# A hybrid decoder layer: a later column addition, last products by halves, and tiles copied by GpSimd's transfers ahead of their transposes

## The chip, the core and the metric

One core of a Trainium2 chip. The time is device microseconds of one launch, the median of the runs shown; one further execution was profiled, and all rows here are from it. Engines are named as in the profile: PE is TensorE's matmuls, PEld its weight loads, DVE VectorE, ACT ScalarE, POOL GpSimd, SP the engine that issues the loads.

## What is computed

One decoder layer on 512 tokens of width 1024, all in float32:

```python
mod = silu(c) @ w_mod + b_mod          # six vectors of 1024: shift, scale, gate, twice
h = rms_norm(x) * (1 + sc_m) + sh_m
proj = h @ w_in                        # q, k, v of two mixers, indexer inputs, two gates
q_a, k_a, q_b, k_b = rope(rms_norm(...))      # 4 heads of 128 each
o_a = attention over the 128 keys that an indexer picks (top-k), causal
o_b = block-sparse attention, causal
merged = sigmoid(gate_a) * (o_a @ w_br_dsa) + sigmoid(gate_b) * (o_b @ w_br_moba)
x = x + gt_m * (merged @ w_out)
h = rms_norm(x) * (1 + sc_f) + sh_f
x = x + gt_f * ((silu(h @ w_gate) * (h @ w_up)) @ w_down)
```

## The kernel before

Products keep float32's precision in three float32r matmuls each: both operands are split into a high and a low part (`wh`, `wl`; tiles of tag `H`, `O`, `K`, `g`), and `mm3` (line 152) adds high x high, high x low and low x high into one PSUM bank. Weights come from DRAM on SP's queue into `st` tiles (`wload`, line 163); ACT makes the high part and DVE the low one.

After the first stage (to about 66 us), the program is written out by a planner that runs when the kernel is built. `Clocks` (line 50) keeps, for each engine, the time that it expects, and for each tile the time at which it should be ready. The main line is a list of chunks of weights (`drive`, line 578; `group`, line 550), whose matmuls go out in a fixed order; after each three of them `step` (line 497) looks at the other tasks, generators that yield what they wait for, and issues what the clocks say is ready by PE's planned time. Engines run their instructions in the order so made, and wait on semaphores where a tile is late in fact.

The tasks that matter here:
- `post` (line 673), one for each of 16 tiles (queries and keys of both mixers, 4 tiles of 128 tokens; tiles `g`): root mean square on ACT, rope on DVE, a power on POOL (`rstd_of`, line 254), the scaling by ACT, 4 transposes on PE by the identity into a PSUM bank (`pstr`), and a copy by ACT into `K`. The tile is float32, and so are its transposes.
- `head` (line 851), one for each mixer, query tile and head: scores (PE, `pss`), mask and maximum (DVE), exponential and scaling (ACT, tile `s`), one to four transposes, a copy (`pT`), the product with the values (`pspv`), and its split (ACT, DVE) into `O`. Mixer 1 (`br` 1) comes first.
- `flip` (line 747) turns the indexer's split tiles: the same transposes, but of float32r tiles, by `identr`.
- `mod_columns` and `columns_task` (lines 959 and 996): four column sums over `w_mod`; each sum lies in a row `K`, goes out to DRAM (`turned`) and comes back as columns of `mcol`. Then one DVE instruction adds the bias to all of them, at a time that the planner takes from its entry for `mcol` plus 8 us.
- `down_done` (line 1317): the last products; the very last accumulator (512 columns) is added to the residual and stored in two halves of 256.

Of the kernel before, what the change touches and what calls it, by code (L numbers as in the profile page):

```python
# [25 lines left out]
P = 128  # L26
# [4 lines left out]
HD = 128  # L31
# [82 lines left out]
def layer(ctx, tc, x, vecs, w_mod, w_in, gvecs, w_br_dsa, w_br_moba, w_out, w_gate_up, w_down, cosh, sinh, cosi, sini, out):  # L114
# [425 lines left out]
    def need_room(tag):  # L540
        pump(lambda: free[tag])
# [5 lines left out]
        if not emptied_next[0]:  # L547
            step()

    def group(srcs, n, accs_of, mm, order, fin, need=(), change=None):  # L550

        accs = {}
        nk = 2 * len(srcs)
        chunks = []
        for c, src in enumerate(srcs):
            def unit(w, ks, js, last, c=c):
                if not accs:
                    accs.update(accs_of())

                held_back[0] = 1.0 if last else 0.0  # L560
                for a, b in ([(k, j) for j in js for k in ks] if last else [(k, j) for k in ks for j in js]):

                    emptied_next[0] = last and a == ks[-1]
                    mm(accs[b], w[0][:, a], w[1][:, a], 2 * c + a, b, c == 0 and a == 0, 2 * c + a == nk - 1)
                    if emptied_next[0]:
                        emptied_next[0] = False
                        fin(b, accs[b])
                        done(accs[b])
                        step()

            last = c == len(srcs) - 1
            h = (len(order) + 1) // 2
            parts = [((0, 1), order[:h]), ((0, 1), order[h:])] if last else [((0,), order), ((1,), order)]
            units = [lambda w, p=p, unit=unit, last=last: unit(w, p[0], p[1], last) for p in parts]
            chunks.append((lambda src=src, n=n: wload(src, 2, n), units, need, change))
        return chunks

    def drive(chunks, ws, ahead=2):
        sts = {}

        def load(c):
            if c < len(chunks) and chunks[c][0]:
                need_room("st")
                sts[c] = chunks[c][0]()

        def prep(c):
            if c < len(chunks) and chunks[c][0]:
                st = sts.pop(c)
                if chunks[c][3]:
                    chunks[c][3](st)  # L590
                yield st
                uid[0] += 1
                h, l = [wp.tile(list(st.shape), F32R, name=f"w{q}_{uid[0]}", tag="w" + q) for q in "hl"]
                se.copy(h, st)
                yield h
                ve.tensor_tensor(out=l, in0=st, in1=h.bitcast(F32), op=ALU.subtract)
                done(st)
                ws[c] = h, l
            load(c + 1)

        load(ahead)
        for c, (load_of, units, need, _) in enumerate(chunks):
            pump(lambda: all(f in ready for f in need) and (not load_of or c in ws))
            for u, unit in enumerate(units):
                unit(ws.get(c))
                if u == 0:
                    spawn(prep(c + ahead), slack=4.0, rank=-1, on=(DVE,))
                    step()
            ws.pop(c, None)
# [60 lines left out]
    tabs = {}  # L670
    qk = {}

    def post(name, g, i, raw):
        if not i:
            yield room("cg", 2), room("K")
            tabs[name] = gain_tables(g)
            qk[name] = t("K", [P, NH, S])
            ready.add("tab" + name)
        yield "tab" + name, raw, room("gu")
        if name == "kb" and i >= 2:  # L680
            yield "idx", room("gu")
        cg, sg = tabs[name]
        ss = small([P, NH])
        for h in range(NH):
            se.activation(sqj, raw[:, h, :], AF.Square, scale=HD ** -0.5, accum_out=ss[:, h:h + 1])
        for _ in rope(raw, cg[:, i:i + 1, :].to_broadcast([P, NH, HD]), sg[:, i:i + 1, :].to_broadcast([P, NH, HD]),
                      NH, HD):
            yield ss, cg, sg
        r = rstd_of(ss, NH)
        yield raw, r  # L690
        for h in range(NH):
            se.activation(raw[:, h, :], raw[:, h, :], AF.Copy, scale=r[:, h:h + 1])
        yield raw, room("pstr")
        pt = ps("tr", (P, NH, P))
        for h in range(NH):
            te.transpose(pt[:, h, :], raw[:, h, :], ident)
        se.copy(qk[name][:, :, i * P:(i + 1) * P], pt)
        done(pt, raw)
        ready.add(f"{name}{i}")
        if all(f"{name}{j}" in ready for j in range(NT)):  # L700
            ready.add(name)
            done(*tabs[name])
            if name == "ka":
                done(cosd, sind, gains)
# [146 lines left out]
    def head(br, i, h):  # L851
        if br:
            yield "qb", "kb", "vb"
            q, k, v, mask = qk["qb"], qk["kb"], vals["vb"], cmask[:, (NT - 1 - i) * P:]
        else:
            yield ("index", "qa", "ka", "va", "started1") + ((f"bias{i}",) if i else ())
            q, k, v, mask = qk["qa"], qk["ka"], vals["va"], bias[i]
        w = (i + 1) * P
        sl = slice(i * P, (i + 1) * P)
        yield q, k, v, mask, room("pss"), room("s")  # L860
        s_ps = ps("s")
        te.matmul(s_ps[:, :w], q[:, h, sl], k[:, h, :w], start=True, stop=True)
        p = t("s", [P, S])
        st = small([P, 4], tag="att")
        nm, z, rz = (st[:, q:q + 1] for q in range(3))

        ve.tensor_tensor_reduce(out=p[:, :w], in0=s_ps[:, :w], in1=mask, op0=ALU.add, op1=ALU.min, scale=-SCALE,
                                scalar=-LOW, accum_out=nm)
        done(s_ps)
        yield st, p  # L870
        se.activation(p[:, :w], p[:, :w], AF.Exp, bias=nm, scale=-1.0, accum_out=z)
        yield p
        ve.reciprocal(rz, z)
        yield st
        se.activation(p[:, :w], p[:, :w], AF.Copy, scale=rz)
        yield p, room("pstr"), room("pT")
        pt = ps("tr")
        for j in range(i + 1):
            te.transpose(pt[:, j * P:(j + 1) * P], p[:, j * P:(j + 1) * P], ident)
        pT = t("pT", [P, S])  # L880
        se.copy(pT[:, :w], pt[:, :w])
        done(pt, p)
        if br not in outs:
            yield room("O", 2)
            outs[br] = [t("O", [P, NH, S], F32R) for _ in range(2)]
            ready.add(f"started{br}")
        yield pT, room("pspv")
        oh, ol = outs[br][0][:, h, sl], outs[br][1][:, h, sl]
        o_ps = ps("pv", (P, P))
        for j in range(i + 1):  # L890
            te.matmul(o_ps, v[:, j, h * HD:(h + 1) * HD], pT[:, j * P:(j + 1) * P], start=(j == 0), stop=(j == i))
        se.copy(oh, o_ps)
        done(pT)
        yield outs[br][0]
        ve.tensor_tensor(out=ol, in0=o_ps, in1=oh.bitcast(F32), op=ALU.subtract)
        done(o_ps)
        heads.remove((br, i, h))
        if not any(b == br for b, _, _ in heads):
            ready.add(f"attn{br}")
            done(vals["vb" if br else "va"], qk["qb" if br else "qa"], qk["kb" if br else "ka"])  # L900
# [58 lines left out]
    def mod_columns(col0):  # L959
# [14 lines left out]
        turned = dp.tile([1, 512], F32, name=f"turned{j0}")  # L974
        nc.sync.dma_start(turned, row)
        nc.sync.dma_start(mcol[:, j0:j0 + 4], turned.rearrange("o (a p) -> p (o a)", p=P), allow_slow_non_contiguous=True)
        arriving(mcol, 512)
        done(tile)

    def mod_rows(acc, col0, tag):  # L980
# [11 lines left out]
        done(pg, *parts)  # L992

    gtm = []

    def columns_task():
        yield "idx"
        for part in range(4):
            yield from mod_columns(3 * D + part * 512)
        landed = ck.ready[mcol.tensor.name][0] + 8.0  # L1000
        yield lambda: landed
        ve.tensor_tensor(out=mcol[:, 24:40], in0=mcol[:, 24:40], in1=bm[:, 24:40], op=ALU.add)
        ve.tensor_scalar(acol[:, 1, :], mcol[:, 32:40], 1.0, None, op0=ALU.add)
        ve.tensor_tensor(out=acol[:, 1, :], in0=acol[:, 1, :], in1=gffn, op=ALU.mult)
# [306 lines left out]
    def gated(half):  # L1311
# [2 lines left out]
            ve.tensor_tensor(out=st, in0=st, in1=gtf[half].unsqueeze(1).to_broadcast([P, 2, 512]), op=ALU.mult)  # L1314
        return change

    def down_done(half):
        def fin(i, acc):
            n = 256 if half and i == NT - 1 else 512
            for a in range(0, 512, n):  # L1320
                cs = slice(half * 512 + a, half * 512 + a + n)
                xs = x1[i // 2][:, i % 2, cs]
                ve.tensor_tensor(out=xs, in0=xs, in1=acc[:, a:a + n], op=ALU.add)
                nc.sync.dma_start(ov[:, i, cs], xs)
        return fin

    for half in range(2):
        hs = slice(half * 512, half * 512 + 512)
        chunks += group([[w_down[k2 * 256:(k2 + 1) * 256, hs]] for k2 in range(NF // 2)], 512,
                        four() if half else other_four, down_mm, [0, 1, 2, 3], down_done(half), change=gated(half))  # L1330

    with tc.manual_schedule(engines=engines):
        start = max(ck.at.values())
# [75 lines left out]
```

## Time and profile before

| | |
|---|---|
| median of 3 runs | 791.69 us (790.19 to 791.88) |
| the profiled execution | 789.93 us |
| its span (first to last instruction) | 787.9 us |
| PE busy | 777.4 us, 99% of the span, 3729 matmuls |
| PEld busy | 646.0 us, 82% |
| DVE busy | 477.3 us, 61% |
| ACT busy | 363.9 us, 46% |
| POOL busy | 30.4 us, 4% |
| share of the DMA engines, loads and stores | 40.2% |
| granted TensorE clock | full (0.999) |

A matmul's row shows more time than it adds: matmuls overlap, and what one costs is the distance from its start to the next start. Idle time of an engine costs only where PE waits for it.

### The profile page before, as it was taken

Reading aid. Unit: us, or ns where it says so; the run is one execution under the profiler, and the core shown is the slowest. Engines: PE = TensorE matmul, PEld = TensorE weight load, DVE = VectorE, ACT = ScalarE, POOL = GpSimd, SP = SyncE. Lnnn points to the kernel's source line nnn. Section 1 sums busy time; section 2 is a strip of 40 time slices with the busy share of each in tenths; the row PEclk is TensorE's granted clock in tenths of the full one; section 3 lists DMA queues with packets and bytes.
Section 4 is the critical chain, followed back from the end, with each engine's and each line's share of the span. In section 5 each row is a group of like instructions: output and inputs, shape, how many; then the busy total and the mean of one; then the engine's idle time right before and its main releaser. Section 6 shows DMA issues by size and latency. Waiting matters only on the chain.

```text
span 787.9 us, 10050 instructions
## 1 busy us (share of the span) xinstructions
PE 777.4 (99%) x3729; PEld 646.0 (82%) x3729; DVE 477.3 (61%) x875; ACT 363.9 (46%) x767; POOL 30.4 (4%) x32
## 2 busy tenths in 40 slices
PE   7999999999999999999999999999999999999998
PEld 6887888887788778888889988888888888888886
DVE  6975889988799586248677365233333334534542
ACT  6763786879876647724446133222332232221210
POOL 2000012101111000000000000000000000000000
PEclk9999999999999999999999999999999999999999
DMA  9976353431235254334621266233333232333311
GB/s 314 354 206 216 94 170 84 158 108 54 80 110 186 74 167 171 138 96 145 189 67 31 64 196 213 85 107 107 97 92 107 84 104 71 117 107 122 118 54 53
DMA packets 80156, 100.61 MB, mean 128 GB/s; under 512 B 8096, under 2 KB 48360, under 8 KB 80108
## 3 DMA queue, kind: packets, MB, share of 16 engines
q1 hardware_dynamic: 80108, 99.98, 40.2%
q8 instruction: 29, 0.48, 0.2%
q14 instruction: 19, 0.16, 0.1%
HBM read 97.86 MB, written 2.11 MB: 127 GB/s over the span
## 4 chain that ended last, share of the span: by engine, by line
PE 97%; DMA 1%; ACT 0%; DVE 0%; SPq 0%; issue 0%; DVEq 0%
PE psacc L107 63%; PE pstr L107 16%; PE pspv L107 9%; PE pss L107 9%; DMA K<-in_w_mod_dram 1%; DMA mcol<-turned 0%; SPq L218 0%; DMA turned<-K 0%; DVE O L107 0%; ACT H L107 0%; ACT s L107 0%; DVE m L107 0%; ACT K L107 0%; SPq L202 0%; DVE V L107 0%
## 5 line engine op out<-in xcount | busy, mean ns | idle before, releaser
L107 DVE TENSOR_TENSOR wl<-st,wh 128x1024 fp32r<-128x1024 f32 (+1 forms) x120 | 144.9, 1209 | 131.9 <-ACT wh L107 131.9
L107 ACT CAST wh<-st 128x1024 fp32r<-128x1024 f32 (+1 forms) x120 | 124.3, 1038 | 172.7 <-PE psacc L107 62.1
L107 PE MATMUL psacc<-H,wh 128*128 128x512 f32 x576 | 183.4, 399 | 0.0
L107 PE MATMUL psacc<-wh,H 128*128 128x512 f32 x384 | 126.3, 400 | 0.2 <-ACT H L107 0.2
L107 PEld LDWEIGHTS psacc<-H,wh 128*128 128x128 f32 x576 | 106.1, 188 | 22.8 <-issue 2.1
L107 PE MATMUL psacc<-H,wl 128*128 128x512 f32 x288 | 112.4, 390 | 0.0
L107 PEld LDWEIGHTS psacc<-wh,H 128*128 128x128 f32 x384 | 72.0, 188 | 15.6 <-ACT H L107 0.7
L107 PE MATMUL psacc<-wl,H 128*128 128x512 f32 x192 | 71.0, 390 | 0.0
L107 PEld LDWEIGHTS psacc<-H,wl 128*128 128x128 f32 x288 | 54.1, 188 | 11.8
L107 PE MATMUL pstr<-H,wh 128*128 128x512 f32 (+1 forms) x176 | 54.3, 390 | 0.0
L107 POOL TENSOR_TENSOR m<-m,mhalf 128x4 f32<-128x4 f32 (+1 forms) x24 | 28.6, 1192 | 393.6 <-DVE m L107 359.6
L107 PEld LDWEIGHTS psacc<-wl,H 128*128 128x128 f32 x192 | 36.2, 188 | 6.8
L107 PE MATMUL psacc<-wh,K 128*128 128x512 f32 x128 | 39.7, 389 | 0.0
L107 PE MATMUL psacc<-O,wh 128*128 128x512 f32 x128 | 39.4, 389 | 0.0
L107 PEld LDWEIGHTS pstr<-H,wh 128*128 128x128 f32 (+1 forms) x176 | 32.3, 183 | 7.6
L107 ACT ACTIVATE s<-s,att 128x256 f32<-128x256 f32 (+3 forms) x64 | 34.0, 563 | 5.4 <-DVE att L107 5.1
L107 DVE TENSOR_TENSOR s<-psacc,s 128x512 f32<-128x512 f32 x12 | 8.3, 692 | 43.2 <-PE psacc L107 43.2
L107 PE MATMUL pstr<-H,wl 128*128 128x512 f32 (+1 forms) x88 | 34.3, 389 | 0.0
L107 ACT ACTIVATE s<-psacc 128x512 f32<-128x512 f32 x12 | 7.2, 598 | 48.0 <-PE psacc L107 48.0
L107 PEld LDWEIGHTS psacc<-O,wh 128*128 128x128 f32 x128 | 24.0, 188 | 5.0
L107 PEld LDWEIGHTS psacc<-wh,K 128*128 128x128 f32 x128 | 24.0, 188 | 5.0
L107 PEld LDWEIGHTS pspv<-pT,V 128*128 128x128 f32 x160 | 22.4, 190 | 6.7 <-DVE O L107 4.0
(234 smaller groups left out, 1360.4 us busy)
## 6 DMA issues: line engine op xcount, KB each, us to landing
st<-in_w_gate_up_dram SPq DMA_DIRECT2D x88, 256.0 KB, 3.2
st<-in_w_in_dram SPq DMA_DIRECT2D x36, 512.0 KB, 3.6
K<-in_w_mod_dram SPq DMA_DIRECT2D x12, 1024.0 KB, 6.3
st<-in_w_down_dram SPq DMA_DIRECT2D x22, 512.0 KB, 3.6
K<-in_w_mod_dram SPq DMA_DIRECT2D x16, 512.0 KB, 5.7
st<-in_w_in_dram SPq DMA_DIRECT2D x16, 256.0 KB, 4.2
st<-in_w_mod_dram SPq DMA_DIRECT2D x8, 512.0 KB, 3.6
O<-in_x_dram SPq DMA_DIRECT2D x4, 512.0 KB, 5.0
```

Source lines behind the costliest of these rows:

```text
L107: inst = f(*args, **kw)
```

## The change

- `columns_task` adds the bias to the columns at a new time: 9.0 us after the later of the planner's DMA clock and the time at which the sums' row is written, instead of the entry of `mcol` plus 8.
- The last accumulator of the last group gets all but its last two k (`full`); those two are multiplied into two banks of 256 columns (`down_end`), and each bank is added and stored by itself.
- Queries and keys (all 16 tiles of `post`) and the softmax weights of mixer 1 (16 of the 32 heads) go through `moved_bits`: a DMA that POOL issues copies the float32 tile, bit for bit, into a float32r tile of tag `g`, and the transposes and `identr` are float32r. The copy's source is freed when it has landed. The planner books 0.6 us of POOL, and a landing 2.6 to 6.1 us after that.
- A `prep` waits until its load has been issued.

```diff
 def post(...):
     for h in range(NH):
         se.activation(raw[:, h, :], raw[:, h, :], AF.Copy, scale=r[:, h:h + 1])
-        yield raw, room("pstr")
-        pt = ps("tr", (P, NH, P))
+        yield raw, room("g")
+        moved = moved_bits(raw)
+        done(raw)
+        yield moved, room("pstr")
+        pt = ps("tr", (P, NH, P), F32R)
         for h in range(NH):
-            te.transpose(pt[:, h, :], raw[:, h, :], ident)
-        se.copy(qk[name][:, :, i * P:(i + 1) * P], pt)
+            te.transpose(pt[:, h, :], moved[:, h * HD:(h + 1) * HD], identr)
+        se.copy(qk[name][:, :, i * P:(i + 1) * P], pt.bitcast(F32))
...
+    def moved_bits(src):
+        dst = t("g", [P, 512], F32R)
+        flat = src.rearrange("p h d -> p (h d)") if len(src.shape) == 3 else src
+        w = flat.shape[-1]
+        nc.gpsimd.dma_start(dst[:, :w].bitcast(F32), flat)
+        pool = mybir.EngineType.Pool
+        issued = max(ck.at.get(pool, 0.0), ck.ready[src.tensor.name][0] + 0.15) + 0.6
+        ck.at[pool] = issued
+        landed = max(issued, min(ck.dma + 1.0, issued + 3.5)) + 2.6
+        ck.ready[dst.tensor.name] = (landed, None)
...
 def head(br, i, h):
+        if br:
+            yield p, room("g")
+            moved, turner, dt = moved_bits(p[:, :w]), identr, F32R
+            done(p)
+        else:
+            moved, turner, dt = p, ident, F32
...
 def mod_columns(col0):
-        arriving(mcol, 512)
+        landed[0] = max(ck.dma, ck.ready[sums.tensor.name][0]) + 9.0
 def columns_task():
-        landed = ck.ready[mcol.tensor.name][0] + 8.0
-        yield lambda: landed
+        yield lambda: landed[0]
...
+    def down_end(w, ks):
+        sl = slice((NT - 1) * P, NT * P)
+        for a, tag in ((0, "pv"), (256, "s")):
+            part = ps(tag, (P, 256))
+            cs = slice(a, a + 256)
+            for n, k in enumerate(ks):
+                mm3(part, act[k][0][:, sl], act[k][1][:, sl], w[0][:, n, cs], w[1][:, n, cs], n == 0, n == len(ks) - 1)
+            add_store(NT - 1, slice(512 + a, 768 + a), part)
```

What this makes of the order. On DVE, the addition to `mcol` and what stands ahead of it. Before (`pss_2926` are scores of a head of mixer 0; on PE they stand four rows behind the matmuls that add up the last column sum):

```order
L107 RECIPROCAL att_2884<-att_2884 128x1
L107 ISA s_2928,att_2929<-pss_2926,score_1075 128x384
L107 ISA att_2929 128x1
L107 MATCH_REPLACE score_1121<-m_8_566_2913,score_1121 128x512
L107 TENSOR_TENSOR mcol<-mcol,cols 128x16
L107 TENSOR_SCALAR acol<-mcol 128x8
L107 TENSOR_TENSOR acol<-acol,cols 128x8
L107 RECIPROCAL att_2908<-att_2908 128x1
```

In the change (`pss_3174` and `pss_3206` are scores of two heads of mixer 0):

```order
L107 ISA s_3176,att_3177<-pss_3174,score_1123 128x512
L107 ISA att_3177 128x1
L107 TENSOR_TENSOR O_2848<-pspv_3161,O_2847 128x128
L107 SCALAR_TENSOR_TENSOR cg_2920<-K_3090,cs,cg_2920 128x512
L107 SCALAR_TENSOR_TENSOR cg_2920<-K_3128,cs,cg_2920 128x512
L107 RECIPROCAL att_3150<-att_3150 128x1
L107 ISA s_3208,att_3209<-pss_3206,score_1123 128x512
L107 ISA att_3209 128x1
L107 TENSOR_TENSOR mcol<-mcol,cols 128x16
L107 TENSOR_SCALAR acol<-mcol 128x8
L107 TENSOR_TENSOR acol<-acol,cols 128x8
```

The addition has moved 41 rows down DVE's list. On PE, 23 rows now stand between the last sum's matmuls and the last scores that DVE treats ahead of it (`pss_3206`), the scores of two other heads among them.

On PE, the transposes of the first three heads of mixer 1 (`s_1730`, `s_1744`, `s_1762` hold their weights; `pss` are scores, `psacc` the main products). Before:

```order
L107 MATMUL pstr_1785<-identr,s_1730 128x128
L107 MATMUL pss_1793<-K_716,K_1322 128x128
L107 MATMUL psacc_1533<-wh_1669,H_105 128x512
L107 MATMUL psacc_1533<-wl_1670,H_105 128x512
L107 MATMUL psacc_1533<-wh_1669,H_107 128x512
L107 MATMUL psacc_1534<-wh_1669,H_105 128x512
L107 MATMUL psacc_1534<-wl_1670,H_105 128x512
L107 MATMUL psacc_1534<-wh_1669,H_107 128x512
L107 MATMUL pspv_1812<-pT_1787,V_844 128x128
L107 MATMUL pstr_1815<-identr,s_1744 128x128
L107 MATMUL pss_1819<-K_716,K_1322 128x256
L107 MATMUL pstr_1824<-identr,s_1762 128x128
```

In the change, where `g_1819`, `g_1837` and `g_1844` are the copies:

```order
L107 MATMUL pstr_1870<-identr,g_1819 128x128
L107 MATMUL pss_1876<-K_716,K_1354 128x128
L107 MATMUL psacc_1815<-wh_1716,H_104 128x512
L107 MATMUL psacc_1815<-wl_1717,H_104 128x512
L107 MATMUL psacc_1815<-wh_1716,H_106 128x512
L107 MATMUL pspv_1892<-pT_1872,V_844 128x128
L107 MATMUL pstr_1895<-identr,g_1837 128x128
L107 MATMUL pstr_1899<-identr,g_1844 128x128
```

From each of these heads' scores to its transposes there were 23, 28 and 20 matmuls; now there are 38, 40 and 34. In the same way the last key tile of mixer 1 (`g_692`) is turned 13 matmuls later, and the second query tile of mixer 1 (`g_1183` before, `g_1176` in the change) 14 later, counted from the last product that made them.

On POOL, from the first power of the tiles on. Before, the powers stand alone:

```order
L107 TENSOR_TENSOR m_4_140_923<-m_4_140_923,mhalf 128x4
L107 TENSOR_TENSOR m_4_158_1045<-m_4_158_1045,mhalf 128x4
L107 TENSOR_TENSOR m_4_159_1050<-m_4_159_1050,mhalf 128x4
L107 TENSOR_TENSOR m_4_196_1240<-m_4_196_1240,mhalf 128x4
L107 TENSOR_TENSOR m_4_228_1391<-m_4_228_1391,mhalf 128x4
L107 TENSOR_TENSOR m_4_229_1396<-m_4_229_1396,mhalf 128x4
```

In the change, with the copies of `g_686`, `g_688`, `g_690` and `g_692`:

```order
L107 TENSOR_TENSOR m_4_140_923<-m_4_140_923,mhalf 128x4
L689 DMA g_1043<-g_686 128x512
L107 TENSOR_TENSOR m_4_159_1047<-m_4_159_1047,mhalf 128x4
L107 TENSOR_TENSOR m_4_160_1052<-m_4_160_1052,mhalf 128x4
L689 DMA g_1130<-g_688 128x512
L689 DMA g_1233<-g_690 128x512
L107 TENSOR_TENSOR m_4_199_1243<-m_4_199_1243,mhalf 128x4
L689 DMA g_1310<-g_692 128x512
```

A copy waits there for ACT's scaling of its source, and the powers behind it wait with it. POOL has 32 copies in all, and the same 24 powers as before.

## Rows read from the trace of the kernel before

**Rows 1.** The page, part 1: busy time, share of the span, instructions.

```profile
PE 777.4 (99%) x3729; PEld 646.0 (82%) x3729; DVE 477.3 (61%) x875; ACT 363.9 (46%) x767; POOL 30.4 (4%) x32
```

**Rows 2.** The table of stretches, its sum over 66 to 783 us.

```profile
sum 717.00, PE 714.73 PEld 594.73 DVE 428.79 ACT 320.25 POOL 25.75; mean PE 119.12 PEld 99.12 DVE 71.46 ACT 53.37 POOL 4.29
```

**Rows 3.** Waits of PE: us in total, times, longest.

```profile
PE pspv L107 <- DVE O L107: 2.3, 1, 2.3
```

**Rows 4.** The timeline near 270 us: start, length, engine, instruction, idle before.

```profile
267.91 0.93 PE L107 MATMUL pstr<-gu,oner 128*2 128x512 f32 x2
...
270.67 0.56 ACT L107 COPY K<-pstr 1x512 f32<-1x512 f32 x1
...
272.40 0.37 SPq L976 DMA_DIRECT2D mcol<-turned  x1
...
274.57 0.17 DVE L107 TENSOR_TENSOR mcol<-mcol,cols 128x16 f32<-128x16 f32 x1 [2.90 <-DMA mcol<-turned]
...
276.07 0.71 PE L107 MATMUL pspv<-pT,V 128*128 128x128 f32 x4 [2.27 <-DVE O L107]
```

**Rows 5.** The chain that ended last: start, length, what.

```profile
724.41 59.85 PE psacc L107 x264
```

**Rows 6.** The timeline of PE around two groups of transposes.

```profile
84.70 0.45 PE L107 MATMUL pstr<-identr,g 128*128 128x128 f32 x4
...
85.29 0.40 PE L107 MATMUL psacc<-wl,H 128*128 128x512 f32 x1
...
123.88 0.60 PE L107 MATMUL pstr<-identr,g 128*128 128x128 f32 x4
...
124.55 0.39 PE L107 MATMUL psacc<-wl,H 128*128 128x512 f32 x1
```

**Rows 7.** The timeline: two pairs of 256-column products, and the end.

```profile
107.44 0.40 PE L107 MATMUL pss<-O 128*128 128x256 f32 x2
107.67 0.41 PE L107 MATMUL pspv<-O 128*128 128x256 f32 x2
...
783.86 0.39 PE L107 MATMUL psacc<-wh,O 128*128 128x512 f32 x1
784.29 0.75 DVE L107 TENSOR_TENSOR V<-V,psacc 128x256 f32<-128x256 f32 x2 [0.67 <-PE psacc L107]
```

**Rows 8.** The timeline: ScalarE scalings and the transposes of the tiles they end.

```profile
121.96 1.29 ACT L107 ACTIVATE g<-g,m 128x128 f32<-128x128 f32 x4
...
144.14 1.29 ACT L107 ACTIVATE g<-g,m 128x128 f32<-128x128 f32 x4
...
146.11 0.60 PE L107 MATMUL pstr<-identr,g 128*128 128x128 f32 x4
...
169.32 0.70 ACT L107 ACTIVATE s<-s,att 128x128 f32<-128x128 f32 x2
...
170.38 0.41 ACT L107 ACTIVATE s<-s,att 128x128 f32<-128x128 f32 x1
...
170.16 0.27 PE L107 MATMUL pstr<-identr,s 128*128 128x128 f32 x1
```

**Rows 9.** DMA issues: count, KB each, median us from issue to landing.

```profile
st<-in_w_gate_up_dram SPq DMA_DIRECT2D x88, 256.0 KB, 3.2
...
out_dram<-V SPq DMA_DIRECT2D x7, 256.0 KB, 2.0
...
K<-in_w_mod_dram SPq DMA_DIRECT2D x7, 1024.0 KB, 7.3
```

**Rows 10.** The timeline of POOL, and VectorE beside the first of them.

```profile
118.70 1.91 POOL L107 TENSOR_TENSOR m<-m,mhalf 128x4 f32<-128x4 f32 x1 [14.26 <-DVE m L107]
...
226.40 1.01 POOL L107 TENSOR_TENSOR m<-m,mhalf 128x4 f32<-128x4 f32 x1 [14.13 <-ACT O L107]
...
118.53 1.22 DVE L107 TENSOR_TENSOR wl<-st,wh 128x1024 fp32r<-128x1024 f32 x1
```

More of the change, by code (lines that the diff above doesn't have):

```diff
@@ L548, in main3, with group @@
             step()
-    def group(srcs, n, accs_of, mm, order, fin, need=(), change=None):
+    def group(srcs, n, accs_of, mm, order, fin, need=(), change=None, end=None):
         accs = {}
@@ L560, in unit @@
                 held_back[0] = 1.0 if last else 0.0
-                for a, b in ([(k, j) for j in js for k in ks] if last else [(k, j) for k in ks for j in js]):
+                pieces = [(k, j) for j in js for k in ks] if last else [(k, j) for k in ks for j in js]
+                if end and last and js[-1] == order[-1]:
+                    del pieces[-len(ks):]
+                for a, b in pieces:
+                    full = nk - 2 if end and b == order[-1] else nk
                     emptied_next[0] = last and a == ks[-1]
-                    mm(accs[b], w[0][:, a], w[1][:, a], 2 * c + a, b, c == 0 and a == 0, 2 * c + a == nk - 1)
+                    mm(accs[b], w[0][:, a], w[1][:, a], 2 * c + a, b, c == 0 and a == 0, 2 * c + a == full - 1)
+                    if end and b == order[-1] and 2 * c + a == full - 1:
+                        fin(b, accs[b], False)
+                        done(accs[b])
                     if emptied_next[0]:
@@ L569, in unit @@
                         step()
+                if end and last and js[-1] == order[-1]:
+                    end(w, [2 * c + a for a in ks])
             last = c == len(srcs) - 1
@@ L587, in prep @@
             if c < len(chunks) and chunks[c][0]:
+                yield lambda: 0.0 if c in sts else None
                 st = sts.pop(c)
@@ L671, in layer @@
     qk = {}
+    def moved_bits(src):
[8 more added lines that the diff above has]
+        ck.ready[dst.tensor.name] = (landed, None)
+        ck.last[src.tensor.name] = (max(ck.last[src.tensor.name][0], landed), None)
+        return dst
     def post(name, g, i, raw):
@@ L692, in post @@
             se.activation(raw[:, h, :], raw[:, h, :], AF.Copy, scale=r[:, h:h + 1])
-        yield raw, room("pstr")
-        pt = ps("tr", (P, NH, P))
+        yield raw, room("g")
[3 more added lines that the diff above has]
+        pt = ps("tr", (P, NH, P), F32R)
         for h in range(NH):
-            te.transpose(pt[:, h, :], raw[:, h, :], ident)
-        se.copy(qk[name][:, :, i * P:(i + 1) * P], pt)
-        done(pt, raw)
+            te.transpose(pt[:, h, :], moved[:, h * HD:(h + 1) * HD], identr)
+        se.copy(qk[name][:, :, i * P:(i + 1) * P], pt.bitcast(F32))
+        done(pt, moved)
         ready.add(f"{name}{i}")
@@ L875, in head @@
         se.activation(p[:, :w], p[:, :w], AF.Copy, scale=rz)
-        yield p, room("pstr"), room("pT")
-        pt = ps("tr")
+        if br:
[4 more added lines that the diff above has]
+            moved, turner, dt = p, ident, F32
+        yield moved, room("pstr"), room("pT")
+        pt = ps("tr", dt=dt)
         for j in range(i + 1):
-            te.transpose(pt[:, j * P:(j + 1) * P], p[:, j * P:(j + 1) * P], ident)
+            te.transpose(pt[:, j * P:(j + 1) * P], moved[:, j * P:(j + 1) * P], turner)
         pT = t("pT", [P, S])
-        se.copy(pT[:, :w], pt[:, :w])
-        done(pt, p)
+        se.copy(pT[:, :w], pt[:, :w].bitcast(F32))
+        done(pt, moved)
         if br not in outs:
@@ L994, in layer @@
     gtm = []
+    landed = [0.0]
     def columns_task():
@@ L1315, in gated, with add_store @@
         return change
-    def down_done(half):
[L1318 to L1325, printed above, removed]
+    def add_store(i, cols, part, store=True):
+        xs = x1[i // 2][:, i % 2, cols]
+        ve.tensor_tensor(out=xs, in0=xs, in1=part, op=ALU.add)
+        if store:
+            nc.sync.dma_start(ov[:, i, cols], xs)
+    def down_done(half):
+        return lambda i, acc, store=True: add_store(i, slice(half * 512, half * 512 + 512), acc, store)
+    def down_end(w, ks):
+        sl = slice((NT - 1) * P, NT * P)
+        for a, tag in ((0, "pv"), (256, "s")):
+            need_room("ps" + tag)
+            part = ps(tag, (P, 256))
[3 more added lines that the diff above has]
+            add_store(NT - 1, slice(512 + a, 768 + a), part)
+            done(part)
     for half in range(2):
@@ L1329, in layer @@
         chunks += group([[w_down[k2 * 256:(k2 + 1) * 256, hs]] for k2 in range(NF // 2)], 512,
-                        four() if half else other_four, down_mm, [0, 1, 2, 3], down_done(half), change=gated(half))
+                        four() if half else other_four, down_mm, [0, 1, 2, 3], down_done(half), change=gated(half),
+                        end=down_end if half else None)
     with tc.manual_schedule(engines=engines):
```

## The prediction

> **What bounds the kernel now.** Read the page first: PE is busy for 777.4 of the 787.9 us span [rows 1]. Then the table of stretches, which says where the rest lies: from 66 to 783 us PE is busy for 714.73 of 717.00 us [rows 2]. All that it idles there is 2.27 us, and the table of waits has it as one wait, of the product with the values for DVE's `O` [rows 3]. The rest of the idle time lies in the first 66 us and behind the last product, so the program's middle is a sum of PE's steps. A step's price is therefore the distance from a matmul's start to the next start, not its length: 264 products of 512 columns in a row take 59.85 us, 0.227 us each [rows 5]. A change pays there only if PE has less to do, or if that one wait goes; a tile that comes late costs its whole lateness.
>
> **The column addition.** The timeline around the wait [rows 4] shows its cause. ACT writes the last row of sums from 270.67 to 271.23 us; the row goes out to DRAM, and its way back is issued at 272.40. DVE stands 2.90 us before the addition to `mcol`, until 274.57. Behind it in DVE's order stand a reciprocal and an `O` that other engines want, and PE resumes at 276.07 after 2.27 us. PE's matmuls for that sum start at 267.91, so from them to the landing 6.6 us pass. In the changed order 23 rows of PE lie between those matmuls and the last scores that DVE treats ahead of the addition; at 0.227 us at least that is 5.2 us, and three scores in that stretch are dearer than a main product, so that DVE comes to the addition some 7 us after the sum or later. Then 2.3 us of wait go. Bounds: 0 if another tile is late at the same place, 2.3 at the most. I take 2.3, since nothing else in 717 us made PE wait.
>
> **The transposes.** 16 tiles of four and mixer 1's 4 x (1 + 2 + 3 + 4): 64 + 40 = 104 transposes change from float32 to float32r. The trace has both kinds in groups of four [rows 6]. At 84.70 is a group of `flip`, float32r: to the second matmul behind it, at 85.29, it is 0.59 us; less one product of 0.227, the group costs 0.363. At 123.88 is one of `post`, float32: 0.67 - 0.227 = 0.443. The planner writes for many kinds of matmul what it believes; what counts is this difference, 0.080 us in four, 0.020 each. So 104 x 0.020 = 2.1 us; I take 2.0, because groups of one to three are not in these rows (bounds: 1.5 if single ones gain half, 2.3). The copies by ACT out of PSUM stay as they were.
>
> **The last products.** Six products of 512 columns (6 x 0.227 = 1.36 us) become twelve of 256; two of these take 107.67 - 107.44 = 0.23 us, so twelve 1.38 us. Before, DVE starts 0.43 us after the last product's start and needs 0.75 us for two halves [rows 7]; now one half, 0.38 us, is left, and a last product of 256 is some 0.1 us shorter, while its start is 0.14 us later. 0.43 + 0.75 - 0.33 - 0.38 - 0.14 = 0.3 us gained. The extra addition of 512 columns on DVE lies in its idle time there, 0.67 us before each addition; without that cover it would cost 0.7.
>
> **The copies.** Each of the 32 tiles now passes through a transfer between ACT and PE. Nothing of it costs PE anything if the tile lands before PE comes to its transposes; the planner has moved these back, so two things set the price: the allowance and the delay.
>
> The allowance is the slack before plus the matmuls moved in between. The last key tile of mixer 1: its scaling ended at 121.96 + 1.29 = 123.25, and PE came at 123.88, 0.63 us later [rows 6, 8]; 13 matmuls more, 2 of them narrow, make 2.5 us: 3.1 us. The second query tile: 144.14 + 1.29 = 145.43, PE at 146.11, 0.68 [rows 8]; 14 matmuls more, of which many are narrow, 2.2 us: 2.9 us. The second head of mixer 1: its scaling ended at 169.32 + 0.41 = 169.73, PE at 170.16, 0.43 [rows 8]; 12 matmuls more, 2.7 us: 3.1 us. The two heads around it wait in the same place and have more. The other tiles, counted in the same way, have over 4 us, many 5 to 10.
>
> The delay is not in the trace, since POOL issues no transfer there. From below: a store of the same 256 KB out of SBUF by SP takes 2.0 us from issue to landing; loads of 256 KB take 3.2 [rows 9]. From above: the 1 MB loads that run in the same stretch take 7.3 us [rows 9]. POOL's own part is unknown: the small powers take it 1.01 us at best [rows 10]. 2.0 + 1.0 = 3.0 to 3.2 + 1.0 = 4.2; I take 3.5, nearer the store, because source and size are the same. Then the three tight places are late by 0.4, 0.6 and 0.4 us: 1.4 us given back. With 3.0 it is 0.1, with 4.2 it is 3.5.
>
> [...]
>
> The copies also stand in POOL's order, and the powers behind them wait with them; each power is wanted by ACT's scaling of its tile. POOL works 25.75 of 717 us [rows 2], so I cost this at nothing; without that idle time it would be about 1 us for each of the 16 powers. Their 7 MB or so lie on DMA engines that PE's weight loads, issued two chunks ahead, do not fill. SP's order keeps its instructions.
>
> **The sum.** -2.3 - 2.0 - 0.3 + 1.4 = -3.2 us against the profiled execution's 789.93 (its span 787.9): 786.7. The median of the runs, 791.69, stands 1.8 us above that execution, and the same difference taken from it gives 788.5. A measurement of this kernel can tell about 0.2% (1.6 us) from no change.
>
> **Rivals.**
> 1. VectorE holds GpSimd off. POOL's power took 1.91 us where it began beside DVE's `wl` subtraction (118.53 to 119.75), and 1.01 elsewhere [rows 10]: 0.9 us of waiting for an instruction with two inputs in SBUF. If the making of a transfer's descriptors waits likewise, the delay is about 3.5 + 0.9 = 4.4; the three places give back 1.3 + 1.5 + 1.3 = 4.1 of the 4.6 us gained: 791.2. For it: DVE is busy with such instructions for much of that stretch. Against: the copy has no operand that POOL itself reads. [...]
> 2. Slower: the copies queue behind the 1 MB loads of `w_mod`. Seven of these lie in the stretch of the copies, each 7.3 us to landing [rows 9], on the same DMA engines. If the tight copies meet them, their delay is that of the loads, 7.3, and they give back 4.2 + 4.4 + 4.2 = 12.8 us: 791.69 - 4.6 + 12.8 = 799.9. It decides from a delay of 4.6 us on, where 3 x 4.6 - 9.1 = 4.6 us eats the whole gain. Against: the planner books up to 3.5 us more where its own DMA clock is late, and the engines are busy for less than half of the time.
> 3. The change doesn't do what it says: a float32r tile that a transfer wrote is turned no faster, or the wait at 274 us only moves to the next late tile. Without the transposes' 2.0 us the sum is -1.2: 790.5; without the wait's 2.3, 790.8. Against: `flip`'s rows are the very instruction.
>
> **How the numbers follow.** Forecast 0.55 (its own range 787.0 to 790.0); rival 1 0.17; rival 2 0.15; rival 3 0.08; 0.05 for all else, spread evenly. Faster by over 0.2% (under 790.1): 0.55 + 0.02 = 0.57. Within: 0.17 + 0.08 + 0.01 = 0.26. Slower (over 793.3): 0.15 + 0.02 = 0.17. The range begins at 785.9 (no tile late, 2.3 us from the transposes, and 0.9 for a low median, as the runs spread) and reaches to 794.5, which takes in rivals 1 and 3 and a delay of 5.5 us at the three places; only the worse part of rival 2 is left out.
>
> **What would show it.** In the trace after: PE's wait for `O` gone and no DVE wait on `mcol<-turned`; the 104 transposes at some 0.09 us from start to start instead of 0.11; one addition behind the last product. Right, for the copies: landings 3 to 4 us after issue, and PE's waits for a `pstr` that end with a DMA, a few tenths each, 1 to 2 us in all. Wrong: landings at 4.6 us or more, and such waits worth over 4 us; or waits of PE on DVE or ACT at places that had none.

## The result: slower, because copies stood behind large loads

The changed kernel takes 796.17 us (median of 6 runs, 794.72 to 799.09) against 790.93 (6 runs, 790.19 to 791.88): 1.0066 times the time before, 95% interval 1.0047 to 1.0084. The forecast was 788.5. Its profiled execution took 794.87 us, its span is 793.1, 5.2 us more than the span before.

The page's first part and the table of stretches (sum over 66 to 789 us) of the changed kernel answer to [rows 1, 2]:

```profile
PE 777.6 (98%) x3735; PEld 645.4 (81%) x3735; DVE 477.8 (60%) x876; ACT 364.8 (46%) x767; POOL 47.8 (6%) x64
```

```profile
sum 723.00, PE 716.05 PEld 594.52 DVE 429.67 ACT 321.30 POOL 43.17; mean PE 716.05 PEld 594.52 DVE 429.67 ACT 321.30 POOL 43.17
```

PE now idles 723.00 - 716.05 = 6.95 us where it idled 2.27 [rows 2]. PE's waits in the changed kernel (us in total, times, longest), to hold against [rows 3]:

```profile
PE pstr L107 <- DMA g<-s: 3.2, 1, 3.2
...
PE pstr L107 <- DMA g<-g: 2.2, 3, 0.9
PE pspv L107 <- DVE O L107: 1.4, 1, 1.4
PE pstr L107 <- DMA K<-in_w_mod_dram: 1.4, 1, 1.4
```

Four waits end with the landing of a copy, 5.4 us in all, and a wait for `O` is still there. (The last row lies in the first stage, whose code is the same; it is 0.6 us before, and up to 1.6 in the other runs.) The first row is the longest of the four; the other three in PE's timeline:

```profile
163.36 0.34 PE L107 MATMUL pstr<-identr,g 128*128 128x128 f32 x2 [0.72 <-DMA g<-g]
...
166.22 0.42 PE L107 MATMUL pstr<-identr,g 128*128 128x128 f32 x3 [0.90 <-DMA g<-g]
...
208.07 0.34 PE L107 MATMUL pstr<-identr,g 128*128 128x128 f32 x2 [0.55 <-DMA g<-g]
```

All 32 copies, as POOL's instructions on tiles `g` (duration in ns, min/median/max; then issue to landing):

```profile
L689 POOL DMA_DIRECT2D g<-g x16: 536/538/727, 99.2 to 249.8; - x16
L689 POOL DMA_DIRECT2D g<-s x16: 534/536/599, 173.9 to 248.0; - x16
...
DMA to landing us min/median/max: 1.8/2.8/7.9
```

POOL needs 0.54 us for one and never more than 0.73. The landings are no single number: taken one by one, 17 of the 32 come within 3.0 us, six after 3.4 to 4.1, two more (256 KB) after 4.5, and seven after 5.5 to 7.9. These seven are the copies issued at 107.6, 157.65, 159.30 and 247.4 to 249.8 us, and each is issued within 3 us of a 1 MB load of `w_mod`. Three of PE's four waits (0.72, 0.90 and 3.21 us) are for copies of these seven. The fourth (0.55) is for the copy issued at 203.45, which landed after 4.5 us though no load was under way (from 203 to 207 us q1, SP's queue, has no packet); why it did is open. Here is the worst place in the timeline:

```profile
246.67 0.71 ACT L107 ACTIVATE s<-s,att 128x512 f32<-128x512 f32 x1
...
247.00 1.01 SPq L952 DMA_DIRECT2D K<-in_w_mod_dram  x2
...
247.38 1.14 POOL L689 DMA_DIRECT2D g<-s  x2
...
254.19 0.72 PE L107 MATMUL pstr<-identr,g 128*128 128x128 f32 x4 [3.21 <-DMA g<-s]
```

The scaling ends at 247.38 and POOL issues the copy at once; the first of the two loads is 0.4 us ahead of it, the second follows at once. What the DMA queues did then (q0 carries POOL's copies, q1 SP's loads; packets, MB, share of 16 engines), first for 247.3 to 250.5 us, with the issues of that stretch (KB each, median us to landing), then for 252 to 254:

```profile
q1 hardware_dynamic: 381, 0.75, 86.4%
...
K<-in_w_mod_dram SPq DMA_DIRECT2D x2, 1024.0 KB, 8.9
g<-s POOLq DMA_DIRECT2D x2, 256.0 KB, 7.1
g<-g POOLq DMA_DIRECT2D x2, 256.0 KB, 7.8
```

```profile
q0 software_dynamic: 120, 0.43, 52.1%
q1 hardware_dynamic: 163, 0.33, 47.1%
```

Until 252 us no packet of the four copies moves: q0 has no line at all in the first stretch (nor has it from 250.5 to 252). The first of the four so waits over 4.6 us for its first packet; the copies issued at 141.03 and 144.02 us, with no 1 MB load near them, have theirs after 1.1 to 1.2. From 252 to 254 us the two queues share the engines by halves (52.1 and 47.1%). The four copies beside these two loads landed after 6.7 us at best.

The wait has a second price, in the granted clock. The table of stretches before, in and behind it (the column ahead of the DMA share is the clock):

```profile
250.90:254.10 3.20, 0.08 (x1) 0.00 (x0) 3.06 (x7) 0.00 (x0) 0.00 (x0) 0.98 0.98 338
254.10:257.40 3.30, 3.20 (x15) 2.84 (x16) 0.39 (x1) 1.16 (x2) 0.00 (x0) 0.50 1.04 407
257.40:302.20 44.80, 44.80 (x237) 35.86 (x237) 33.52 (x97) 30.59 (x84) 0.00 (x0) 1.00 0.48 155
```

PE stands for 3.2 us, then works 3.3 us at a clock of 0.50. Two main products take 0.97 us there (254.72 to 255.69) and 0.45 at a clock of 1.00 (160.21 to 160.66), so PE does half of what it could: about 1.6 us more, an estimate from the 3.3 us.

The two prices that were read from single places came out as foreseen (what all 104 transposes gave stands under f4_rounded). PE's timeline around the last key tile's transposes, to hold against [rows 6]:

```profile
126.88 0.46 PE L107 MATMUL pstr<-identr,g 128*128 128x128 f32 x4
...
127.47 0.40 PE L107 MATMUL psacc<-wl,H 128*128 128x512 f32 x1
```

0.59 us from the group to the second matmul behind it, 0.67 before. And the end, to hold against [rows 7]:

```profile
788.31 0.28 PE L107 MATMUL pspv<-wh,O 128*128 128x256 f32 x1
...
789.62 0.28 PE L107 MATMUL pss<-wh,O 128*128 128x256 f32 x1
789.94 0.42 DVE L107 TENSOR_TENSOR V<-V,pss 128x256 f32<-128x256 f32 x1 [0.29 <-PE pss L107]
```

From the start of the last k's products (before, six of 512 columns, 5 x 0.227 us ahead of 783.86) to the end of DVE's last addition it was 784.29 + 0.75 - 782.73 = 2.31 us; it is 789.94 + 0.42 - 788.31 = 2.05 now.

The `O` wait has another cause than before. The changed kernel's timeline near 300 us:

```profile
291.73 0.24 SPq L1010 DMA_DIRECT2D turned<-K  x1
...
295.15 0.38 SPq L1011 DMA_DIRECT2D mcol<-turned  x1
...
295.62 5.09 SPq L952 DMA_DIRECT2D K<-in_w_mod_dram  x3
...
301.16 0.75 DVE L107 SCALAR_TENSOR_TENSOR cg<-K,cs,cg 128x512 f32<-128x512 f32 x1 [2.59 <-DMA K<-in_w_mod_dram]
...
302.50 0.17 DVE L107 TENSOR_TENSOR mcol<-mcol,cols 128x16 f32<-128x16 f32 x1
...
304.46 0.71 PE L107 MATMUL pspv<-pT,V 128*128 128x128 f32 x4 [1.42 <-DVE O L107]
```

DVE comes to the addition (302.50) without a wait, as forecast. But SP holds its list for the row's way back until 295.15, the `w_mod` load behind it is late, and DVE waits 2.59 us for that: 1.42 of the 2.27 us come back on PE.

### The profile page after: what moved, and what is told of

Read it like the earlier page. It is cut to its first block, busy times and chain, and to the rows that moved or that the text cites. A ratio compares the mean times of both kernels' runs of the same rounds, so it can differ in the third digit from the quotient of the medians.

```text
span 793.1 us, 10167 instructions
## 1 busy us (share of the span) xinstructions
PE 777.6 (98%) x3735; PEld 645.4 (81%) x3735; DVE 477.8 (60%) x876; ACT 364.8 (46%) x767; POOL 47.8 (6%) x64
## 4 chain that ended last, share of the span: by engine, by line
PE 90%; DMA 4%; DVE 2%; ACT 2%; POOL 1%; issue 1%; SPq 0%; DVEq 0%; POOLq 0%
PE psacc L107 58%; PE pstr L107 15%; PE pss L107 8%; PE pspv L107 8%; DMA K<-in_w_mod_dram 2%; DMA g<-g 1%; DMA g<-s 1%; POOL m L107 1%; DMA turned<-K 0%; ACT g L107 0%; DVE g L107 0%; DVE wl L107 0%; ACT s L107 0%; DVE score L107 0%; SPq L218 0%
## 5 line engine op out<-in xcount | busy, mean ns | idle before, releaser
L107 ACT CAST wh<-st 128x1024 fp32r<-128x1024 f32 (+1 forms) x120 | 124.4, 1037 | 175.1 <-PE psacc L107 63.4
L107 ACT ACTIVATE s<-s,att 128x128 f32<-128x128 f32 (+3 forms) x64 | 34.7, 561 | 3.5 <-DVE att L107 3.5
L107 DVE TENSOR_TENSOR st<-st,cg 128x1024 f32<-128x1024 f32 x22 | 26.8, 1218 | 0.0
```

Of the source, the lines that this page charges most:

```text
L107: inst = f(*args, **kw)
```

## The experiments

Each ran beside the kernel before on the same chip; the median of that was 791.56 us (e), 792.0 (f) and 791.43 (g). Chips differ by some tenths of a us, so runs of different letters are better compared by their ratios. The expectations count a copy's delay to the first sign of its landing (2.0 to 2.3 alone, 4.5 to 7 late); the rows here count to the last (1.8 to 3.0, and 5.5 to 7.9).

| run | what | median us | ratio, 95% interval |
|---|---|---|---|
| e1_late | before + later addition | 788.7 | 0.9970 [0.9955, 0.9985] |
| e2_halves | before + halves at the end | 791.05 | 0.9993 [0.9979, 1.0008] |
| e3_moves | before + copies | 799.4 | 1.0102 [1.0083, 1.0121] |
| e4_nomoves | changed kernel - copies | 787.59 | 0.9946 [0.9931, 0.9962] |
| f1_sums_later | changed kernel, sums later | 800.16 | 1.0101 [1.0086, 1.0116] |
| f2_nomoves_sums_later | f1 - copies | 795.65 | 1.0054 [1.0041, 1.0068] |
| f3_act_queue | copies issued by ACT | 808.96 | 1.0215 [1.0203, 1.0228] |
| f4_rounded | float32r tiles without copies | 787.42 | 0.9949 [0.9935, 0.9964] |
| g1_hold | two loads held behind four copies | 791.21 | 0.9998 [0.9984, 1.0011] |
| g2_booked | late copies booked as late | 790.5 | 0.9999 [0.9985, 1.0013] |
| g3_partial | 25 copies only | 795.86 | 1.0057 [1.0040, 1.0074] |
| g4_after_again | the changed kernel | 796.87 | 1.0063 [1.0048, 1.0078] |

### The parts alone

**e1_late.** The addition's hunks alone:

```diff
-        arriving(mcol, 512)
+        landed[0] = max(ck.dma, ck.ready[sums.tensor.name][0]) + 9.0
...
-        landed = ck.ready[mcol.tensor.name][0] + 8.0
-        yield lambda: landed
+        yield lambda: landed[0]
```

> The kernel before with the later column addition alone. Theory (the wait at the addition goes and nothing takes its place): the 2.27 us of PE's wait for O at 274 us are gone, 788.7 us against 790.93. Rival (the row's way out and back still holds SP's queue, the w_mod loads behind it land late and DVE waits for those, as the changed kernel shows with 2.6 us of DVE and 1.4 us of PE at 303 us): 0.85 us gained, 790.1. Second rival (the addition was never what cost time): 790.9.

788.7 us against 791.56: the whole wait of 2.27 us goes, and from 66 us on PE has no wait left. (The gain is 0.6 us more than the wait; in some executions a stretch at half clock follows that wait, as the last section shows.) The step was right by itself. What comes back of it in the changed kernel comes with the copies: without them, in e4_nomoves below, there is no such wait.

**e2_halves.** The hunks of `group`, `down_end` and `down_done` alone:

```diff
-        chunks += group(..., down_mm, [0, 1, 2, 3], down_done(half), change=gated(half))
+        chunks += group(..., down_mm, [0, 1, 2, 3], down_done(half), change=gated(half),
+                        end=down_end if half else None)
```

> The kernel before with the last products by halves alone. Theory: 0.3 to 0.4 us gained at the end, 790.6, with one addition of 0.38 us behind the last product. Rival (the extra addition of 512 columns or the two short banks cost as much as they save): 790.9 to 791.6.

791.05 against 791.56: 0.5 us less, which the interval can't tell from nothing. The rows of the end above show 0.3.

**e3_moves.** `moved_bits` and its two uses, with the wait in `prep`, and nothing else:

```diff
+        moved = moved_bits(raw)
+        done(raw)
...
-            te.transpose(pt[:, h, :], raw[:, h, :], ident)
+            te.transpose(pt[:, h, :], moved[:, h * HD:(h + 1) * HD], identr)
```

> The kernel before with the copies by GpSimd's transfers alone (and the wait of a preparation for its load, which the planner then needs). Theory (the copies are what lost the time: most land 2.0 to 2.3 us after their issue, those that start behind a 1 MB load of w_mod land 4.5 to 7 us after it; PE waits for them for 4 to 6 us and then runs some 3 us at the half clock; the transposes give back 1.2 to 2.0): 794 to 797, with PE's waits on a copy at the places where a w_mod load stands just ahead. Rival (the loss in the changed kernel comes of the three changes together, or of the column addition's new place): 789 to 791, waits on copies under 1.5 us in all.

799.4, the theory's side and 2.4 us above its range: PE waits for copies at three of the changed kernel's four places, and the old wait for `O` is there on top. Behind the two longest (3.4 and 2.6 us) this execution has the clock at 0.50, from 256.3 to 259.6 us and from 300.7 to 304.0.

```profile
PE pstr L107 <- DMA g<-s: 3.4, 1, 3.4
...
PE pspv L107 <- DVE O L107: 2.6, 1, 2.6
PE pstr L107 <- DMA g<-g: 2.1, 2, 1.3
```

**e4_nomoves.** The reverse: the changed kernel with `post` and `head` as they were.

```diff
-        moved = moved_bits(raw)
-        done(raw)
...
-            te.transpose(pt[:, h, :], moved[:, h * HD:(h + 1) * HD], identr)
+            te.transpose(pt[:, h, :], raw[:, h, :], ident)
```

> The changed kernel without the copies: later column addition and last products by halves. Theory (the copies alone lost the time): faster than the kernel before by the sum of the two parts, 788.3 if the whole wait of 2.27 us goes, 789.7 if 1.4 us of it comes back at the w_mod loads. Rival (the column addition's new place is what lost time): 791 or more.

787.59 us, faster than both kernels: 0.9946 times the time before. PE has no wait from 66 us to the end (its sum over 66 to 782 us):

```profile
sum 716.00, PE 716.00 PEld 595.57 DVE 429.49 ACT 320.24 POOL 25.78; mean PE 716.00 PEld 595.57 DVE 429.49 ACT 320.24 POOL 25.78
```

So the loss comes with the copies: with them the kernel stands at 1.0066 of the time before, without them at 0.9946, some 9 us apart.

### Why the copies are late

**g1_hold** leaves every engine's order as it is, and adds two small instructions on POOL behind its last four copies, on whose tiles the two loads of the fourth sum must then wait:

```diff
                 tile = t(tag, [P, n, 512])
+                if tag == "K" and acc is None and col0 == 3 * D + 1536:
+                    nc.gpsimd.memset(tile[:, 0, 0:2], 0.0)
```

> The changed kernel in the very same order, with one addition: GpSimd clears two columns of each of the two 1 MB tiles of the fourth column sum, behind its last four copies, so that these two loads can only be issued after the copies. Theory (the copies are late because those loads are ahead of them on the DMA engines): the last four copies land 2 to 4 us after issue instead of 6 to 7, PE's wait of 3.2 us at 254 us and the 3.4 us of half clock behind it (1.7 us) go: 4.9 us less than the changed kernel run beside it. Rival (whatever else is at work in that stretch, GpSimd or VectorE, makes them late): no change. Second rival (the loads, now late by some 4 us, make DVE late and PE waits there): 0 to 2 us less.

791.21 us beside 796.87 for the changed kernel on the same chip, 5.7 less; 4.9 were expected. The timelines of POOL and of SP in that run:

```profile
249.02 1.14 POOL L689 DMA_DIRECT2D g<-s  x2
250.15 0.54 POOL L689 DMA_DIRECT2D g<-g  x1
251.43 0.54 POOL L689 DMA_DIRECT2D g<-g  x1 [0.74 <-ACT g L107]
251.96 0.15 POOL L952 MEMSET K<- 128x2 f32 x2
```

```profile
252.11 1.02 SPq L954 DMA_DIRECT2D K<-in_w_mod_dram  x2
```

and its DMA issues from 248.5 to 252 us, with the landings:

```profile
g<-s POOLq DMA_DIRECT2D x2, 256.0 KB, 3.3
g<-g POOLq DMA_DIRECT2D x2, 256.0 KB, 3.7
```

7.1 and 7.8 us have become 3.3 and 3.7, the 3.2 us wait is gone, and PE's clock there is full (1.00 from 250 to 258 us). The same copies, issued by the same engine beside the same work of VectorE, are on time when the loads come second. For these four copies, which held PE longest, that is the cause shown, and it rules out VectorE. The three late copies at 107 to 160 us are still late in g1_hold (5.5 to 7.6 us; PE waits 1.60 us for one at 164.67 and 0.82 at 167.47), beside loads that were not held.

**f3_act_queue** has ACT issue the copies:

```diff
-        nc.gpsimd.dma_start(dst[:, :w].bitcast(F32), flat)
+        nc.scalar.dma_start(dst[:, :w].bitcast(F32), flat)
```

> The changed kernel, with the 32 copies issued by ACT instead of GpSimd, in the same places of the order. Theory (a copy waits on the DMA engines behind the 1 MB loads, whoever issues it): the copies at about 108, 158, 159 and 247 to 250 us land 4.5 to 7 us after their issue as before, PE waits 4 to 6 us for them, 793 to 797. Rival (GpSimd is slow to write its descriptors, or VectorE holds it off): all land within 2 to 3 us and the waits go, 786 to 788.

The delays are those expected: alone 2.3, beside the two loads 7.0. The DMA issues of 126 to 156 us, and of 261.5 to 266:

```profile
g<-g ACTq DMA_DIRECT2D x3, 256.0 KB, 2.3
```

```profile
g<-s ACTq DMA_DIRECT2D x1, 256.0 KB, 7.0
```

So beside the loads a copy is as late when ACT issues it. (The trace tells the landing of 19 of the 32.) The time was a miss, 808.96 where 793 to 797 stood: PE waits 13.9 us for copies, at eight places. Three of those waits (2.4 to 2.5 us each, one of them the wait at 120.44) are for copies that landed within 2.4 us of their issue; ACT came to issue them late. For the one at 120.44 the timeline shows why: the scaling of its tile begins at 110.42 and takes 1.30 us, and ACT's list has over ten other instructions between it and the copy, issued at 118.05; POOL had issued the same copy (at 111.23 in the changed kernel) 0.3 us behind the scaling.

**f1_sums_later** and **f2_nomoves_sums_later** were to take the loads out of the copies' stretch:

```diff
 def columns_task():
-        yield "idx"
+        yield "idx", "attn1"
```

> The changed kernel, with the column sums over w_mod begun only when all heads of mixer 1 are out, so that no 1 MB load stands near a copy. Theory (a copy is late where it starts behind a 1 MB load, and nowhere else): every copy lands 1.7 to 4 us after its issue, PE's waits on copies fall from 5.4 us to under 1, and the time is that of the run without copies (787.6) less 1.2 to 2.0 for the transposes: 785.6 to 786.4, if the later sums bring no wait of their own. Rival (VectorE's instructions hold GpSimd off): DVE has as much to do beside the copies, so the same tiles stay late: 795 or more.

> The control for it: without the copies, the column sums as late. If the sums' place is worth nothing by itself, 787.6 as without the copies and with the sums at their old place; if the 1 MB loads or DVE's part of the sums held PE in other ways, 785 to 787; if they now press on the addition to mcol, 788 to 790.

Both missed. f1's 800.16 us lies where its rival put it, but not for the rival's reason: its late copies stand behind 1 MB loads again, as shown below. Without copies the later sums cost 8 us by themselves (795.65 against 787.59), a wait for weights that DVE makes too late among them:

```profile
PE psacc L107 <- DVE wl L107: 3.1, 1, 3.1
```

And in f1 SP runs ahead of PE's plan: the first two loads are out before the last four copies, and the first of these lands after 8.4 us, the longest delay of all. Its timeline:

```profile
233.69 0.92 SPq L952 DMA_DIRECT2D K<-in_w_mod_dram  x2
...
234.91 0.60 POOL L689 DMA_DIRECT2D g<-g  x1 [4.21 <-ACT g L107]
...
243.41 0.72 PE L107 MATMUL pstr<-identr,g 128*128 128x128 f32 x4 [3.94 <-DMA g<-g]
```

What the two show: the three copies that were late at 107 to 160 us beside a load now take 2.3 to 4.8 us, and PE's waits there are 0.17 + 0.47 = 0.64 us instead of 0.72 + 0.90 = 1.62. As a version it is useless.

### Can the copies be made to pay?

**f4_rounded** asks what the transposes are worth without any copy. ACT's scaling writes the float32r tile; queries, keys and mixer 1's weights are rounded on the way, which leaves out the exact bits.

```diff
-            se.activation(raw[:, h, :], raw[:, h, :], AF.Copy, scale=r[:, h:h + 1])
-        yield raw, room("g")
-        moved = moved_bits(raw)
+            se.activation(moved[:, h * HD:(h + 1) * HD], raw[:, h, :], AF.Copy, scale=r[:, h:h + 1])
```

> The changed kernel without any copy: ACT's scaling writes the float32r tile itself. This leaves out the exact bits (queries, keys and mixer 1's weights are rounded on the way), and shows what the 104 float32r transposes give back by themselves. Theory: 2.0 us (0.019 each) less than the run without copies and with float32 transposes: 785.6. Rival (transposes are hidden in part, or other distances grow): 786.2 to 787.6.

787.42 us, at the rival's upper end. f4 and e4 ran on different chips and their runs differ in mean clock, so the traces say more than the medians (787.42 and 787.59). Both have full clock from one and the same product behind the first stage (at 67.23 us in e4, 70.03 in f4) to the start of the last one. PE is busy there for all of e4's 715.82 us, and in f4 for:

```profile
sum 714.80, PE 714.40 PEld 593.91 DVE 429.81 ACT 320.52 POOL 24.01; mean PE 714.40 PEld 593.91 DVE 429.81 ACT 320.52 POOL 24.01
```

The transposes give 715.82 - 714.40 = 1.4 us, not 2.0, and a new wait of PE takes 0.4 of it back.

**g2_booked** tells the planner what the trace showed, by the copy's number:

```diff
-        landed = max(issued, min(ck.dma + 1.0, issued + 3.5)) + 2.6
+        copies[0] += 1
+        landed = issued + BOOK.get(copies[0], 2.6)
...
+    BOOK = {1: 5.2, 6: 4.6, 7: 5.7, 28: 6.1, 29: 6.6, 30: 7.0, 31: 6.8}
```

> The changed kernel with the planner told the delays that its trace shows: 4.6 to 7.0 us for the seven copies that met a 1 MB load, 2.6 for the others. Theory (only the booked delay was wrong): PE's waits on copies fall under 1 us, and the time is 786 to 788, the run without copies less about 1 us for the transposes. Rival (in the new order other copies meet the loads, which a constant cannot know): waits of 2 us or more at other tiles, 790 to 796.

790.5 us, 6.4 less than the changed kernel beside it; so much came of the order that the true delays make, in which the wait for `O` is gone too. But the time is the rival's. In the new order six copies start within 3.5 us of one another (190.3 to 193.8), beside two loads of 512 KB, and PE waits for one that was booked at 2.6 and landed after 5.1:

```profile
PE pstr L107 <- DMA g<-s: 1.7, 1, 1.7
```

**g3_partial** copies only the 25 tiles that had been on time:

```diff
+        if (name, i) in [('kb', 1), ('qb', 2), ('qb', 3), ('ka', 2), ('ka', 3)]:
+            moved, turner, dt = raw.rearrange("p h d -> p (h d)"), ident, F32
...
```

(and heads 2 and 3 of the last query tile in the same way.)

> The changed kernel with copies only for the 25 tiles that met no 1 MB load; the other seven keep their float32 transposes. Theory: waits on copies under 1 us, 786.5 to 788. Rival (the order shifts and other copies meet the loads): 790 or more.

795.86 us, the rival again: a copy that had been on time starts beside the loads of the fourth sum, lands after 6.1 us, and PE waits 2.4; and 3.3 us are lost at another head.

```profile
PE pss L107 <- DVE att L107: 3.3, 1, 3.3
...
PE pstr L107 <- DMA g<-s: 2.4, 1, 2.4
```

**g4_after_again.**

> The changed kernel once more, on the same chip as the three beside it: 794.7 to 799, as measured before.

796.87, as before. No version with copies beat e4_nomoves, the best of those that keep the exact bits.

## Why the prediction was wrong

The terms, forecast against the profiled execution:

| term | forecast | measured |
|---|---|---|
| wait at the column addition | -2.3 | -2.27 + 1.42 = -0.85 |
| 104 transposes | -2.0 | -1.4 (f4_rounded) |
| last products | -0.3 | -0.3 |
| late copies | +1.4 | 3.21 + 0.90 + 0.72 + 0.55 = +5.4 |
| half clock behind the longest wait | not foreseen | +1.6 |
| a wait of the first stage | not foreseen | 1.4 - 0.6 = +0.8 |
| sum | -3.2 | +5.2 (the spans: +5.2) |

1. **The step that failed is the delay.** "I take 3.5, nearer the store, because source and size are the same" gave one delay to 32 copies. A copy alone was in fact cheaper: 2.2 to 2.3 us for 256 KB (those issued at 144.02 and 141.03). But seven copies of 32 took 5.5 to 7.9, each issued within 3 us of a 1 MB load; for four of them g1_hold shows that it came of the loads (7.1 and 7.8 us became 3.3 and 3.7). The term stood at +1.4 and measured +5.4, and the prediction's own sign of being wrong came in: landings over 4.6 us, and waits on them worth over 4.
2. **The allowances were used at the wrong places.** The three tight tiles (copies issued at 122.8, 144.0 and 175.1 us) landed after 2.7, 2.2 and 2.6, and PE waited for none. Late were tiles that the text put at "over 4 us" and left out: the third and fourth query tile of mixer 1 and a head of its last tile. That one had 254.19 - 3.21 - 247.38 = 3.6 us.
3. **Rival 2 had the mechanism**, "the copies queue behind the 1 MB loads", and its delay of 7.3 us stands in the rows. It got 0.15 because "the planner books up to 3.5 us more where its own DMA clock is late". That does not happen in this program: with the planner's clocks printed while the kernel is built, its DMA clock lies 1.8 to 24.8 us behind the copy's issue at all 32, so it books 2.6 for each. The two loads of the fourth sum it books only behind the last four copies, as ending at 243.9 and 246.9 us; SP issues them at 247.0 and 247.5, the first 0.4 us ahead of the first of these copies. And its price, 12.8 us, came of putting the delay at the three tight tiles. (Its turning point is off by a little: 3 x 4.6 - 9.1 is 4.7.)
4. **Rival 1 fell.** POOL took 0.53 to 0.73 us for each of the 32 copies, and the last four copies of g1_hold were on time beside the same VectorE work. The copy issued at 249.79 in the changed kernel took POOL 0.54 us beside DVE's `wl` subtraction (249.58 to 250.79).
5. **The addition was right, alone.** e1_late has the whole 2.27 us. In the changed kernel "0 if another tile is late at the same place" is what partly happened, through SP's list: behind the row's way back stands a load that DVE wants.
6. **The transposes** were priced from one group, 0.080 us. The same tile measured 0.08, but the whole came to 1.4 us (f4_rounded), 0.014 each.
7. **The clock was left out.** A wait was priced at its own length. The longest one, 3.21 us, cost half as much again (about 1.6).
8. The 1.8 us between the profiled execution before and the median go with the clock too: of 23 runs of the kernel before beside the last group, five had a mean clock of 0.999 and a median of 789.39, eleven had 0.997 and 791.54. The profiled execution (789.93) had no stretch at half clock between 66 us and its last product. That such stretches make the whole difference is not shown.

## What to carry to other kernels

A transfer's delay was no constant of its kind here: 256 KB took 2.2 us alone and 6.7 to 7.9 beside two 1 MB loads. So look at what else the DMA engines carry when it is issued, and price it once alone and once behind the largest load that can be ahead of it. A queue that ran ahead (here SP's, by 0.4 us) put its loads in front of transfers that the planner had booked first; where a small transfer is urgent, let the large load wait for it, as g1_hold does (3.3 and 3.7 us instead of 7.1 and 7.8). Where PE is never idle, a late tile costs its lateness (5.4 us of waits here), and behind the wait of 3.21 us came 3.3 us at half clock on top.

## What was not expected of the hardware

- A copy issued between two 1 MB loads did not get a packet through for over 4.6 us, while q0 and q1 shared the engines evenly later (52.1 and 47.1%). The delay was the same (7.0 us) when ACT issued it. Why its packets began so late no run here shows.
- The clock fell to 0.50 behind PE's wait of 3.21 us, and in e3_moves behind waits of 3.42 and 2.58 us. A wait of 2.3 us had it behind it in one execution and not in another, and behind g3_partial's wait of 3.32 us no slower stretch is seen: from 296.46 us two main products take 0.54 us, as they do from 299.04. The same stretch behind the wait for `O`, in e2_halves and in the kernel before (the column ahead of the DMA share is the clock):

```profile
278.50:281.90 3.40, 3.40 (x9) 2.46 (x8) 2.60 (x8) 2.08 (x6) 0.00 (x0) 0.50 0.04 11
```

```profile
278.50:281.90 3.40, 3.40 (x19) 2.67 (x18) 3.40 (x9) 1.47 (x5) 0.00 (x0) 1.00 0.18 19
```

9 matmuls against 19. So a wait of PE of 2.3 to 3.4 us did not always bring the stretch; what decides it no run here shows.
